# Gate stage woven with a longer row of dense matmuls, and query and key projections in two passes over the tokens, in a two-layer attention and mLSTM encoder

## The chip, the cores and the metric

The kernel runs on one core of one Trainium2 chip. The metric is the device time of one execution in microseconds (us). The core's engines work side by side, each through its own list of instructions in a fixed order: PE (matrix products, with PEld for the loads of its stationary operand), DVE and ACT (elementwise work), POOL, and SP, which here issues DMA transfers. An instruction that waits holds back everything behind it on its engine.

## The reference

Two batches, 256 sample tokens and 512 prompt tokens, pass through two layers with shared weights. Each layer runs differential attention and a bidirectional mLSTM side by side on one input projection, then an output projection, a layer norm, and a gated feed-forward part with a second layer norm. The part that matters here:

```python
aq, ak, av, lq, lk, lv, lo, lg = _split_cols(x @ w_in)
att = _diff_attention(aq, ak, av, lam)                     # 4 heads, 2 score maps each
gates = (lg + gate_bias).reshape(B, S, 4, LSTM_HEADS)
ig_f, lf_f = gates[0], jax.nn.log_sigmoid(gates[1])        # forward; gates 2 and 3 backward
h = _mlstm_direction(q, k, v, ig_f, lf_f) + (same, flipped in time)
mixed = concat([att, sigmoid(lo) * head_rmsnorm(h)]) @ w_out
```

`_mlstm_direction` needs, from the gates, running sums and running maxima along the tokens (a scan), per chunk of 128 tokens.

## The kernel before

All 768 tokens lie in one activation tile, `actA`, the 256 sample tokens first, in six token tiles of 128. Each fp32 product is made of three passes over a high and a low part, so one tile of a dense projection with 1024 input features is 8 x 3 = 24 matmuls.

A layer's first half, the mixer, goes through these stages:

- `lstm_in`: the projections of the mLSTM's queries, keys and gates (`c1a`, `c1b`).
- `gates`: a long chain of small steps, nearly all on DVE and ACT. PE comes in three times: it transposes the gate values (`gT`, L474), spreads 64 values over partitions with a small product (`aB`, L517), and transposes the results back (`colT`, L524, four groups).
- `dense("av")`: the attention's values, six tiles of 24 matmuls of 512 columns. `dense("lv")` and `dense("lo")` are of the same form, for the mLSTM's values and output gates.
- `att_in(h)`: query and key projection of head h. `feat_major` (L347) makes 24 pairs of matmuls, each with one stationary weight block: 256 columns for the sample tokens (into `aqkB`), 512 for the prompt tokens (into `aqkA`). One PSUM tile `pB` holds the sample part of the queries in its first half and of the keys in its second.
- `att(h)`: per block of 128 queries two score products (`s`), a reduction on DVE, two exponentials on ACT, a combination on DVE, transposes (`aT`) and the product with the values (`u`).
- `lstm_states` and `lstm_out`: the mLSTM proper. `lstm_decay` loads the decay tiles `pt` (L570) and `qet` (L577) from DRAM through SP, after the gate stage has written their source there, adds a mask on DVE (L572) and takes exponentials on ACT (L574).

What stands beside what is written by hand. `weave` takes one step (up to the next `yield`) of the generator that is least far along, by the step counts given to it:

```python
weave((gates(), 8), (dense("av", ev_av), 7))
weave((att_in(0), 3))
weave((att(0), 7, PR_A), (dense("lv", ev_lv), 7, PR_LO))
```

The framework's scheduler then makes each engine's final order from this program order and the priorities. Weights come as raw pieces (`raw`, six buffers), and are converted into two parts (`wh` on ACT, L171; `wl` on DVE, L172) in twelve slots. A conversion waits until the last matmul that used its slot is done, and the load of a raw piece waits until the piece that had its buffer is converted.

Of the kernel before, what the change touches and what calls it, by code (L numbers as in the profile page):

```python
# [20 lines left out]
SA, SB = 512, 256  # L21
T = SA + SB
# [24 lines left out]
PR_A = 0  # L47
PR_L = 0
PR_LO = 10
# [156 lines left out]
def trunk(ctx, nc, tc, d, o, depth=DEPTH):  # L206
    V, S, G, PE = nc.vector, nc.scalar, nc.gpsimd, nc.tensor
# [18 lines left out]
    def P(tag, name):  # L226
        return pp.tile([128, 512], F32, tag=tag, name=name, bufs=banks[tag])
# [118 lines left out]

    def feat_major(blocks, psA, psB):  # L347

        n = 0
        for k in range(8):  # L350
            _, h, l = blocks[k // 4]
            for a, b in PASSES:
                w = (h, l)[a][:, (k % 4) * 128:(k % 4 + 1) * 128]
                PE.matmul(psB, w, actA[:, k, b, 0:SB], start=n == 0, stop=n == 23)  # L354
                PE.matmul(psA, w, actA[:, k, b, SB:T], start=n == 0, stop=n == 23)  # L355
                n += 1

    def transposed_split(src, name, tag, hi, lo):

# [8 lines left out]
    for l in range(depth):  # L368
# [28 lines left out]
        def dense(tag, evac):  # L397
            units = [W.take() for _ in range(8)]
            for t in range(NT):
                p = P("d", f"{tag}{t}")  # L400
                tok_major(t, units, p, slice(0, 512))
                evac(t, p)
                yield
            W.done(*units)
# [23 lines left out]
        def gates():  # L428
# [38 lines left out]
            t2 = gp.tile([128, T], F32, name="t2")  # L467
            mpe = gp.tile([64, 2, 6], F32, name="mpe")
            ae = gp.tile([64, 6], F32, name="ae")
            for c0, c1 in ((0, 4), (4, 6)):  # L470
                ps = P(TAG_GT, f"gT{c0}")
                n = (c1 - c0) * 128
                for t in range(c0, c1):
                    PE.transpose(ps[:, (t - c0) * 128:(t - c0 + 1) * 128], gs[:, t].rearrange("p a b c -> p (a b c)"), ident)  # L474
                S.copy(ig[:, c0 * 128:c1 * 128], ps[0:64, :n])
                V.tensor_copy(lf[:, c0 * 128:c1 * 128], ps[64:128, :n])
# [35 lines left out]
            V.tensor_tensor(out=v6(t2[64:128]), in0=v6(t1[0:64]), in1=me.unsqueeze(2).to_broadcast([64, 6, 128]), op=ALU.subtract)  # L512
            V.tensor_tensor(out=ae, in0=mp, in1=me, op=ALU.subtract)
            S.activation(ae, ae, AF.Exp)
            ps = P(TAG_GT, "aB")
            for i in range(4):
                PE.matmul(ps[:, i * 6:(i + 1) * 6], sel[:, i, :], ae, start=True, stop=True)  # L517
# [148 lines left out]
        def att_in(h):  # L666
            qs = 0.125 * 2.0 ** (8.0 * (h + 1) / 4)
            uq, uk = [[W.take(), W.take()] for _ in range(2)]
            pB = P("d", f"aqkB{h}")
            lo_, hi_ = slice(0, 64), slice(64, 128)  # L670
            for ui, uu in ((0, uq), (1, uk)):
                pA = P("d", f"aqkA{h}{ui}")
                pBu = pB[:, ui * 256:(ui + 1) * 256]
                feat_major(uu, pA, pBu)
                W.done(*uu)
                for ps, tk in ((pBu, slice(0, SB)), (pA, slice(SB, T))):
                    if ui == 0:
                        S.activation(sQ[lo_, 0, tk], ps[lo_], AF.Identity, scale=qs)
                        S.activation(sQ[hi_, 1, tk], ps[hi_], AF.Identity, scale=qs)
                        V.scalar_tensor_tensor(out=sQ[hi_, 0, tk], in0=ps[lo_], scalar=qs, in1=sQ[lo_, 0, tk].bitcast(F32), op0=ALU.mult, op1=ALU.subtract)  # L680
                        V.scalar_tensor_tensor(out=sQ[lo_, 1, tk], in0=ps[hi_], scalar=qs, in1=sQ[hi_, 1, tk].bitcast(F32), op0=ALU.mult, op1=ALU.subtract)
                    else:
                        S.copy(sK[lo_, 0, tk], ps[lo_])
                        S.copy(sK[hi_, 1, tk], ps[hi_])
                        S.copy(sK[hi_, 0, tk], ps[lo_])
                        S.copy(sK[lo_, 1, tk], ps[hi_])
                        V.tensor_tensor(out=kL[lo_, 0, tk], in0=ps[lo_], in1=sK[lo_, 0, tk].bitcast(F32), op=ALU.subtract)
                        V.tensor_tensor(out=kL[hi_, 1, tk], in0=ps[hi_], in1=sK[hi_, 1, tk].bitcast(F32), op=ALU.subtract)
                yield
# [49 lines left out]
        def weave(*gens):  # L739

            live = [[0, n, i, g, (*o, 0)[0]] for i, (g, n, *o) in enumerate(gens)]
            while live:
                e = min(live, key=lambda e: ((e[0] + 0.5) / e[1], e[2]))
                e[0] += 1
                with prio(e[4]):
                    done = next(e[3], live) is live
                if done:
                    live.remove(e)

        def chain(*gens):  # L750
            for g in gens:
                yield from g
# [3 lines left out]
            late_constants()  # L756
        G.iota(dneg, [[-1, 896]], base=384, channel_multiplier=1, allow_small_or_imprecise_dtypes=True)
        V.scalar_tensor_tensor(out=dneg, in0=dneg, scalar=-1.0, in1=dneg, op0=ALU.mult, op1=ALU.min)
        weave((gates(), 8), (dense("av", ev_av), 7))
        CPX = ExitStack()  # L760
        lc = CPX.enter_context(tc.tile_pool(name=f"lc{l}", bufs=1, reuse_waits="tile"))
        weave((att_in(0), 3))
        weave((att(0), 7, PR_A), (dense("lv", ev_lv), 7, PR_LO))
        lo = dense("lo", ev_lo)
        weave((chain(att_in(1), att(1)), AT1, PR_A), (chain(lstm_states(lc), *[lstm_out(lc, c) for c in range(OUTS)]), 4 * OUTS + 9, PR_L), *([(islice(lo, L1), L1 + W1)] if L1 else []))
        weave((chain(att_in(2), att(2)), AT2, PR_A), (chain(*[lstm_out(lc, c) for c in range(OUTS, NT)]), 4 * (NT - OUTS) + 1, PR_L), *([(islice(lo, L2), L2 + W2, PR_LO)] if L2 else []))
# [331 lines left out]
```

## Time and profile before

| | |
|---|---|
| three runs | 1855.55, 1855.73 (median), 1857.43 us |
| profiled execution | 1855.45 us, of which 1853.7 us are the span of the trace |
| busy share | PE 97%, PEld 86%, DVE 72%, ACT 41%, POOL 13% |
| granted PE clock over the span | 0.992 |
| chain that ended last, by engine | PE 78%, DVE 13%, ACT 5% |

The profiled execution is one of the same kernel, 0.3 us below the median of the runs. The span runs from the first to the last instruction; the remaining 1.75 us lie around it. A clock of 1.00 is PE's upper level, 2.4 GHz; the lower level, 1.2 GHz, would show as 0.50, and a window's figure is the mean over it.

### The profile page before, as it was taken

How to read it: one execution, taken by the hardware profiler on the slowest of the kernel's cores; microseconds unless marked ns; L12 is line 12 of the kernel's file. 1: busy time of each engine (PE TensorE's matmuls, PEld its weight loads, DVE VectorE, ACT ScalarE, POOL GpSimd, SP SyncE). 2: the span in 40 equal slices, each digit the busy share in tenths (PEclk: the TensorE clock that was granted, in tenths of full speed). 3: DMA queues.
4: the chain of work that ended last, by engine and by line, in shares of the span. 5: the costliest groups of instructions: out<-in, count | busy, mean ns of one | idle time of the engine just before them, and what ended most of it. 6: DMA issues, size and time to landing. Idle time of an engine off the chain costs nothing.

```text
span 1853.7 us, 26256 instructions
## 1 busy us (share of the span) xinstructions
PE 1804.3 (97%) x9692; PEld 1587.1 (86%) x9692; DVE 1340.4 (72%) x2576; ACT 768.9 (41%) x1624; POOL 241.9 (13%) x260
## 2 busy tenths in 40 slices
PE   8899999999999999999998999999999999999998
PEld 8778777789899899899897787777898998998996
DVE  5434787589887786787954457775898877877878
ACT  4344576425343343343332455672353343343340
POOL 2000111041111111110120011011411111111102
PEclk9999999999999999999999999999999999999999
DMA  6232110402322222122322121104022221221211
GB/s 190 67 79 69 35 58 24 159 18 69 92 74 69 64 74 68 64 75 86 101 96 83 42 69 52 46 25 170 2 90 80 80 79 47 80 76 51 80 63 68
DMA packets 83280, 134.95 MB, mean 73 GB/s; under 512 B 7984, under 2 KB 27056, under 8 KB 83152
## 3 DMA queue, kind: packets, MB, share of 16 engines
q1 hardware_dynamic: 82432, 132.90, 22.7%
q8 instruction: 76, 1.25, 0.3%
q14 instruction: 52, 0.43, 0.1%
q10 hardware_dynamic: 720, 0.37, 0.1%
HBM read 126.86 MB, written 6.39 MB: 72 GB/s over the span
## 4 chain that ended last, share of the span: by engine, by line
PE 78%; DVE 13%; ACT 5%; issue 2%; POOL 2%; DMA 1%; SPq 0%; DVEq 0%; ACTq 0%; POOLq 0%
PE p L921 32%; PE dn L981 16%; PE wo L877 5%; PE aqkA L355 3%; PE lv L345 3%; PE lo L345 3%; PE aqkB L354 2%; DVE wl L172 2%; PE c1a L345 2%; PE u L724 2%; PE av L345 2%; PE c1b L345 2%; PE num L618 1%; ACT wh L171 1%; PE num L614 1%
## 5 line engine op out<-in xcount | busy, mean ns | idle before, releaser
L921 PE MATMUL p<-actA,wh 128*128 128x384 f32 x1408 | 363.4, 338 | 3.2 <-DVE g L946 3.2
L171 ACT ACTIVATE wh<-raw 128x512 fp32r<-128x512 f32 (+1 forms) x348 | 215.5, 629 | 303.3 <-PE p L921 110.2
L172 DVE TENSOR_TENSOR wl<-raw,wh 128x512 fp32r<-128x512 f32 (+1 forms) x348 | 243.2, 708 | 96.9 <-ACT wh L171 96.4
L921 PE MATMUL p<-actB,wh 128*128 128x384 f32 x1056 | 270.0, 337 | 0.0
L921 PEld LDWEIGHTS p<-actA,wh 128*128 128x128 f32 x1408 | 254.7, 188 | 5.8 <-DVE g L946 3.8
L921 PE MATMUL p<-actA,wl 128*128 128x384 f32 x704 | 237.3, 337 | 0.0
L149 POOL TENSOR_TENSOR T<-raw,raw 128x512 f32<-128x512 f32 x88 | 120.5, 1371 | 837.0 <-DVE wl L172 525.7
L981 PE MATMUL dn<-wh,actB 128*128 128x512 f32 x576 | 208.8, 396 | 1.1 <-DVE acc L988 1.1
L171 ACT ACTIVATE wh<-T 128x512 fp32r<-128x512 f32 x176 | 108.4, 628 | 221.3 <-DVE acc L988 104.9
L921 PEld LDWEIGHTS p<-actB,wh 128*128 128x128 f32 x1056 | 191.3, 188 | 0.0
L981 PE MATMUL dn<-wh,ring 128*128 128x512 f32 x480 | 179.1, 396 | 1.6 <-DVE acc L988 1.6
L921 PE MATMUL p<-actB,wl 128*128 128x384 f32 x528 | 177.2, 336 | 0.0
L988 DVE TENSOR_TENSOR acc<-acc,dn 128x512 f32<-128x512 f32 x144 | 98.1, 681 | 72.0 <-PE dn L981 71.7
L172 DVE TENSOR_TENSOR wl<-T,wh 128x512 fp32r<-128x512 f32 x176 | 129.6, 748 | 22.0 <-ACT wh L171 21.9
L981 PEld LDWEIGHTS dn<-wh,actB 128*128 128x128 f32 x576 | 108.0, 188 | 29.8 <-DVE acc L988 2.8
L921 PEld LDWEIGHTS p<-actA,wl 128*128 128x128 f32 x704 | 132.2, 188 | 0.1
L877 PE MATMUL wo<-wh,actB 128*128 128x512 f32 x384 | 122.7, 396 | 0.0
L981 PE MATMUL dn<-wl,actB 128*128 128x512 f32 x288 | 113.2, 393 | 0.0
L981 PEld LDWEIGHTS dn<-wh,ring 128*128 128x128 f32 x480 | 90.0, 188 | 24.6 <-DVE acc L988 4.2
L921 PEld LDWEIGHTS p<-actB,wl 128*128 128x128 f32 x528 | 99.1, 188 | 0.0
L355 PE MATMUL aqkA<-actA,wh 128*128 128x512 f32 x256 | 98.8, 408 | 0.0
L981 PE MATMUL dn<-wl,ring 128*128 128x512 f32 x240 | 94.5, 394 | 0.0
(265 smaller groups left out, 3412.5 us busy)
## 6 DMA issues: line engine op xcount, KB each, us to landing
raw<-in_w_g_dram SPq DMA_DIRECT2D x88, 256.0 KB, 2.8
raw<-in_w_u_dram SPq DMA_DIRECT2D x88, 256.0 KB, 2.8
raw<-in_w_down_dram SPq DMA_DIRECT2D x88, 256.0 KB, 2.8
raw<-in_w_out_dram SPq DMA_DIRECT2D x32, 256.0 KB, 2.6
pt<-scr_m SPq DMA_DIRECT2D x12, 512.0 KB, 6.2
raw<-in_w_c_dram SPq DMA_DIRECT2D x16, 264.0 KB, 3.6
raw<-in_w_av_dram SPq DMA_DIRECT2D x16, 256.0 KB, 4.1
raw<-in_w_aq_dram SPq DMA_DIRECT2D x16, 256.0 KB, 3.7
```

Of the source, the lines that this page charges most:

```text
L149: src["engine"].tensor_tensor(out=src["tile"], in0=a, in1=b, op=ALU.subtract)
L171: self.nc.scalar.activation(h, v, AF.Identity)
L172: self.nc.vector.tensor_tensor(out=l, in0=v, in1=h.bitcast(F32), op=ALU.subtract)
L345: PE.matmul(ps, xh(k, t, a), (h, l)[b][:, cols], start=k + i == 0, stop=k == 7 and i == 2)
L354: PE.matmul(psB, w, actA[:, k, b, 0:SB], start=n == 0, stop=n == 23)
L355: PE.matmul(psA, w, actA[:, k, b, SB:T], start=n == 0, stop=n == 23)
L614: PE.matmul(pn[:, di * 256:di * 256 + 129], qet[r, di, hh // 2, :], cst[di, c][r, hh // 2, :], start=di == dirs[0], stop=False, skip_group ...
L724: PE.matmul(pu[:, qt * 128:(qt + 1) * 128], aT[:, st * 128:(st + 1) * 128], av[:, s0 + st, h * 128:(h + 1) * 128], start=st == 0, stop=st ...
L877: PE.matmul(p, actB[:, k, a, t * 128:(t + 1) * 128], units[k][1 + b], start=n + i == 0, stop=n == 7 and i == 2)
L921: PE.matmul(ps, blk[1 + a][:, k * 128:(k + 1) * 128], x[:, k, b, :], start=k + i == 0, stop=k == 3 and i == 2)
L981: PE.matmul(p, x, (wh_, wl_)[b], start=k + i == 0, stop=k == nf - 1 and i == 2)
L988: V.tensor_tensor(out=z, in0=z, in1=p, op=ALU.add)
```

## The change

`feat_major` makes two passes: first the 24 matmuls of the sample tokens, then the 24 of the prompt tokens, with the same stationary blocks in the same order. `gates` gets two more `yield`s, one ahead of the `gT` transposes and one ahead of `aB`. Its partner in the weave is now a chain: all of `av`, then `att_in(0)`, then the first tile of `lv`. The next weave has what is left of `lv`, five tiles. The pool `lc`, in which the decay tiles lie, is still opened after the gate stage's pool is closed, which is now after `att_in(0)` in program order.

```diff
--- before.py
+++ after.py
@@ -346,14 +346,14 @@
 
     def feat_major(blocks, psA, psB):
 
-        n = 0
-        for k in range(8):
-            _, h, l = blocks[k // 4]
-            for a, b in PASSES:
-                w = (h, l)[a][:, (k % 4) * 128:(k % 4 + 1) * 128]
-                PE.matmul(psB, w, actA[:, k, b, 0:SB], start=n == 0, stop=n == 23)
-                PE.matmul(psA, w, actA[:, k, b, SB:T], start=n == 0, stop=n == 23)
-                n += 1
+        for ps, tok in ((psB, slice(0, SB)), (psA, slice(SB, T))):
+            n = 0
+            for k in range(8):
+                _, h, l = blocks[k // 4]
+                for a, b in PASSES:
+                    w = (h, l)[a][:, (k % 4) * 128:(k % 4 + 1) * 128]
+                    PE.matmul(ps, w, actA[:, k, b, tok], start=n == 0, stop=n == 23)
+                    n += 1
 
     def transposed_split(src, name, tag, hi, lo):
 
@@ -467,6 +467,7 @@
             t2 = gp.tile([128, T], F32, name="t2")
             mpe = gp.tile([64, 2, 6], F32, name="mpe")
             ae = gp.tile([64, 6], F32, name="ae")
+            yield
             for c0, c1 in ((0, 4), (4, 6)):
                 ps = P(TAG_GT, f"gT{c0}")
                 n = (c1 - c0) * 128
@@ -512,6 +513,7 @@
             V.tensor_tensor(out=v6(t2[64:128]), in0=v6(t1[0:64]), in1=me.unsqueeze(2).to_broadcast([64, 6, 128]), op=ALU.subtract)
             V.tensor_tensor(out=ae, in0=mp, in1=me, op=ALU.subtract)
             S.activation(ae, ae, AF.Exp)
+            yield
             ps = P(TAG_GT, "aB")
             for i in range(4):
                 PE.matmul(ps[:, i * 6:(i + 1) * 6], sel[:, i, :], ae, start=True, stop=True)
@@ -756,11 +758,11 @@
             late_constants()
         G.iota(dneg, [[-1, 896]], base=384, channel_multiplier=1, allow_small_or_imprecise_dtypes=True)
         V.scalar_tensor_tensor(out=dneg, in0=dneg, scalar=-1.0, in1=dneg, op0=ALU.mult, op1=ALU.min)
-        weave((gates(), 8), (dense("av", ev_av), 7))
+        lv = dense("lv", ev_lv)
+        weave((gates(), 10), (chain(dense("av", ev_av), att_in(0), islice(lv, 1)), 10))
         CPX = ExitStack()
         lc = CPX.enter_context(tc.tile_pool(name=f"lc{l}", bufs=1, reuse_waits="tile"))
-        weave((att_in(0), 3))
-        weave((att(0), 7, PR_A), (dense("lv", ev_lv), 7, PR_LO))
+        weave((att(0), 7, PR_A), (lv, 6, PR_LO))
         lo = dense("lo", ev_lo)
         weave((chain(att_in(1), att(1)), AT1, PR_A), (chain(lstm_states(lc), *[lstm_out(lc, c) for c in range(OUTS)]), 4 * OUTS + 9, PR_L), *([(islice(lo, L1), L1 + W1)] if L1 else []))
         weave((chain(att_in(2), att(2)), AT2, PR_A), (chain(*[lstm_out(lc, c) for c in range(OUTS, NT)]), 4 * (NT - OUTS) + 1, PR_L), *([(islice(lo, L2), L2 + W2, PR_LO)] if L2 else []))
```

No instruction is added or taken away on any engine; the change is one of order, and it reaches from the gate stage to the start of the output projection (`wo`) in each layer. Both layers get the same order, but for a few rows (before, 19 of the 24 matmuls of the first `av` tile stood ahead of `gT` in layer 0, and 22 in layer 1; now all 24 do in both). The places below are those of layer 0.

**First place: PE in the gate stage, at `aB`.** `av2`, `av3`, `av4` are tiles of the value projection. Before:

```order
L345 MATMUL av2_784<-wl25_573,actA_70 128x512
L345 MATMUL av2_784<-wh25_572,actA_70 128x512
L345 MATMUL av2_784<-wh26_578,actA_70 128x512
L517 MATMUL aB_778<-ae_686,sel_636 128x6 x4
L345 MATMUL av2_784<-wl26_579,actA_70 128x512
L345 MATMUL av2_784<-wh26_578,actA_70 128x512
L345 MATMUL av2_784<-wh27_584,actA_70 128x512
```

and after:

```order
L345 MATMUL av3_804<-wh28_590,actA_70 128x512
L345 MATMUL av3_804<-wl28_591,actA_70 128x512
L345 MATMUL av3_804<-wh28_590,actA_70 128x512
L519 MATMUL aB_830<-ae_686,sel_636 128x6 x4
L345 MATMUL av4_836<-wh21_188,actA_70 128x512
L345 MATMUL av4_836<-wl21_189,actA_70 128x512
L345 MATMUL av4_836<-wh21_188,actA_70 128x512
```

Before, `aB` stands inside the third value tile, after 16 of its 24 matmuls; now it stands between the fourth and the fifth, and the `gT` transposes, which were inside the first and second tile, come after the first and inside the second.

**Second place: PE in the projections of head 0.** `aqkA00` and `aqkA01` are the prompt parts of queries and keys, `aqkB0` the tile with both sample parts; the suffixes of wh and wl name weight blocks. Before, at the step from queries to keys:

```order
L354 MATMUL aqkB0_962<-actA_70,wh30_602 128x256
L355 MATMUL aqkA00_963<-actA_70,wh30_602 128x512
L354 MATMUL aqkB0_962<-actA_70,wl30_603 128x256
L355 MATMUL aqkA00_963<-actA_70,wl30_603 128x512
L355 MATMUL aqkA01_1032<-actA_70,wh31_608 128x512 x2
L355 MATMUL aqkA01_1032<-actA_70,wl31_609 128x512
L355 MATMUL aqkA01_1032<-actA_70,wh31_608 128x512 x2
L355 MATMUL aqkA01_1032<-actA_70,wl31_609 128x512
L355 MATMUL aqkA01_1032<-actA_70,wh31_608 128x512
L354 MATMUL aqkB0_962<-actA_70,wh31_608 128x256 x2
```

and after, at the step from the sample pass to the prompt pass of the queries:

```order
L355 MATMUL aqkB0_949<-actA_70,wl30_603 128x256
L355 MATMUL aqkB0_949<-actA_70,wh30_602 128x256 x2
L355 MATMUL aqkB0_949<-actA_70,wl30_603 128x256
L355 MATMUL aqkA00_950<-actA_70,wh29_596 128x512 x2
L355 MATMUL aqkA00_950<-actA_70,wl29_597 128x512
L355 MATMUL aqkA00_950<-actA_70,wh29_596 128x512 x2
```

Before, sample and prompt matmuls alternate and both tiles end together; now the sample tile ends 24 prompt matmuls earlier. The keys' sample pass follows the queries' prompt pass, and the first `lv` tile follows the keys' prompt pass as a whole (before, the first scores stood inside it).

**Third place: ACT and SP around the decay tiles.** ACT before:

```order
L171 ACTIVATE wh41_1012<-raw41_926 128x512
L574 ACTIVATE pt0_1834<-pt0_1834,cols_239 128x128 x5
L678 ACTIVATE sQ_228<-aqkB0_962 64x256
L679 ACTIVATE sQ_228<-aqkB0_962 64x256
L678 ACTIVATE sQ_228<-aqkA00_963 64x512
L679 ACTIVATE sQ_228<-aqkA00_963 64x512
L171 ACTIVATE wh42_1018<-raw42_932 128x512
L574 ACTIVATE pt0_1834<-pt0_1834,cols_239 128x128 x3
L171 ACTIVATE wh43_1081<-raw43_938 128x512
L574 ACTIVATE pt1_1856<-pt1_1856,cols_239 128x128 x8
```

and ACT after, where `tp000` are the exponentials of the first attention block:

```order
L533 ACTIVATE cols_239<-colT41_1096 128x2x8 x2
L576 ACTIVATE pt0_1834<-pt0_1834,cols_239 128x128 x5
L412 COPY vaug_237<-lv0_1101 128x4x128
L576 ACTIVATE pt0_1834<-pt0_1834,cols_239 128x128
L716 ACTIVATE tp000_1135,sm000_1134<-tp000_1135,mn000_1136 128x256
L716 ACTIVATE tp000_1135,cc000_1137<-tp000_1135,mn000_1136 128x256
L576 ACTIVATE pt0_1834<-pt0_1834,cols_239 128x128 x2
L576 ACTIVATE pt1_1856<-pt1_1856,cols_239 128x128 x7
L724 COPY aT000_1154<-aT000_1151 128x256
```

The decay exponentials stood between two key conversions and ahead of the evacuation of the queries (`sQ`); now they stand behind both projections and ahead of the first attention block. DVE's order has moved in the same way: the two mask additions of `pt0` stand directly ahead of the reductions of `tp000`, and the first of `pt1` between these and the combination that `aT000` waits for.

SP's list of DMA transfers, before:

```order
L140 DMA raw45_950<-in_w_aq_dram 128x512
L140 DMA raw46_956<-in_w_aq_dram 128x512
L570 DMA pt0_1834<-scr_m 128x8x128
L577 DMA qet0_1846<-scr_e 64x4x128 x2
L140 DMA raw47_1016<-in_w_ak_dram 128x512
L570 DMA pt1_1856<-scr_m 128x8x128
```

and after:

```order
L140 DMA raw46_947<-in_w_aq_dram 128x512
L140 DMA raw47_1003<-in_w_ak_dram 128x512
L140 DMA raw48_1009<-in_w_ak_dram 128x512
L140 DMA raw49_1076<-in_w_lo_dram 128x512
L572 DMA pt0_1834<-scr_m 128x8x128
L140 DMA raw50_1082<-in_w_lo_dram 128x512
L579 DMA qet0_1846<-scr_e 64x4x128 x2
L572 DMA pt1_1856<-scr_m 128x8x128
```

The load of `pt0` stood behind `raw46` and now stands behind `raw49`, and `pt1` behind `raw50` and both loads of `qet0`.

## Rows read from the trace of the kernel before

**Rows 1.** The page, part 1: busy time of each engine, its share, its instructions.

```profile
PE 1804.3 (97%) x9692; PEld 1587.1 (86%) x9692; DVE 1340.4 (72%) x2576; ACT 768.9 (41%) x1624; POOL 241.9 (13%) x260
```

**Rows 2.** Busy time by window: span, busy (count) per engine, PEclk, DMA, GB/s.

```profile
90.60:114.00 23.40, 19.97 (x100) 17.14 (x98) 8.24 (x14) 10.01 (x29) 0.00 (x0) 0.85 0.63 164
161.40:240.00 78.60, 78.19 (x487) 63.23 (x487) 51.45 (x151) 41.00 (x119) 9.96 (x13) 1.00 0.21 64
240.00:337.00 97.00, 94.27 (x546) 75.17 (x544) 76.10 (x230) 70.25 (x206) 11.52 (x14) 1.00 0.14 44
1012.20:1036.00 23.80, 21.31 (x108) 17.77 (x107) 9.56 (x17) 12.58 (x34) 0.00 (x0) 0.93 0.59 163
```

**Rows 3.** Waits of PE, layer 0, 45 to 340 us: total, times, longest.

```profile
PE aB L517 <- ACT ae L514: 5.3, 1, 5.3
PE aqkB L354 <- DVE sQ L681: 3.4, 1, 3.4
```

**Rows 4.** Waits of PE, layer 1, 966 to 1262 us.

```profile
PE aqkB L354 <- DVE sQ L681: 2.4, 1, 2.4
PE gT L474 <- DVE gs L461: 1.2, 1, 1.2
```

**Rows 5.** Timeline of PE, layer 0: start, length, engine, line, operation, [idle before].

```profile
45.19 0.40 PE L345 MATMUL av<-wh,actA 128*128 128x512 f32 x1
...
50.55 0.63 PE L474 MATMUL gT<-ident,gs 128*128 128x128 f32 x4 [0.80 <-DVE gs L461]
50.94 0.48 PE L345 MATMUL av<-wl,actA 128*128 128x512 f32 x1
...
67.11 1.84 PE L517 MATMUL aB<-ae,sel 64*128 64x6 f32 x8 [5.26 <-ACT ae L514]
...
69.47 1.05 PE L345 MATMUL av<-wh,actA 128*128 128x512 f32 x2
...
113.97 0.39 PE L345 MATMUL lv<-wh,actA 128*128 128x512 f32 x1
```

**Rows 6.** Timeline of PE, layer 1.

```profile
966.81 0.39 PE L345 MATMUL av<-wh,actA 128*128 128x512 f32 x1
...
989.80 1.84 PE L517 MATMUL aB<-ae,sel 64*128 64x6 f32 x8 [5.25 <-ACT ae L514]
...
1033.25 0.40 PE L345 MATMUL lv<-wh,actA 128*128 128x512 f32 x1
```

**Rows 7.** The chain of work that ended last: start, length, step.

```profile
36.64 2.84 PE c1b L345 x24
...
73.28 5.55 PE av L345 x24
...
93.04 7.22 DMA pt<-scr_m
```

**Rows 8.** Timeline of DVE, layer 0.

```profile
51.83 0.69 DVE L476 COPY lf<-gT 64x512 f32<-64x512 f32 x1 [1.43 <-ACT ig L475]
...
100.39 1.29 DVE L572 TENSOR_TENSOR pt<-pt,tri 128x512 f32<-128x512 f32 x2 [4.22 <-DMA pt<-scr_m]
```

**Rows 9.** Timeline of ACT, layer 0.

```profile
66.75 0.21 ACT L514 ACTIVATE ae<-ae 64x6 f32<-64x6 f32 x1
...
101.16 1.57 ACT L574 ACTIVATE pt<-pt,cols 128x128 f32<-128x128 f32 x5 [5.72 <-DVE pt L572]
...
118.27 0.51 ACT L714 ACTIVATE tp<-tp,mn 128x256 f32<-128x256 f32 x1
```

**Rows 10.** The page, parts 5 and 6: weight conversions, loads of the decay tiles.

```profile
L171 ACT ACTIVATE wh<-raw 128x512 fp32r<-128x512 f32 (+1 forms) x348 | 215.5, 629 | 303.3 <-PE p L921 110.2
L172 DVE TENSOR_TENSOR wl<-raw,wh 128x512 fp32r<-128x512 f32 (+1 forms) x348 | 243.2, 708 | 96.9 <-ACT wh L171 96.4
...
pt<-scr_m SPq DMA_DIRECT2D x12, 512.0 KB, 6.2
```

**Rows 11.** Timeline of SP's DMA queue, layer 0.

```profile
93.52 1.73 SPq L577 DMA_DIRECT2D qet<-scr_e  x2
```

## The prediction

> **What bounds the kernel now.** The page comes first: PE is busy for 97% of the span and DVE for 72% [rows 1]. A change of order can only gain where PE stands still or runs at a lower clock, so the next view is the list of PE's waits in each mixer. In layer 0 it has two large entries: 5.3 us at `aB`, behind the exponential on ACT that ends the gate chain, and 3.4 us at the keys' sample matmul, behind DVE's evacuation of the queries [rows 3]. Layer 1 has the same places with 5.25 us [rows 6] and 2.4 us, and 1.2 us at `gT` [rows 4]. The windows show the second cost. The projections of head 0 ran at a mean clock of 0.85 in layer 0 and 0.93 in layer 1 [rows 2], so part of each window, after the wait, was at 1.2 GHz. After the wait at `aB` it is the same: two 512-column matmuls take 1.05 us [rows 5], where an undisturbed tile of 24 takes 5.55 us, 0.231 each [rows 7]. The later mixer is nearly full: PE is busy 78.19 of 78.60 us and 94.27 of 97.00 us [rows 2]. What can be gained lies between the first `av` matmul and the first `lv` matmul.
>
> How much, follows from that stretch as a whole. It lasts 113.97 - 45.19 = 68.8 us in layer 0 [rows 5] and 1033.25 - 966.81 = 66.4 us in layer 1 [rows 6]. Its PE work is the same before and after: six `av` tiles of 5.55 us are 33.3; two projections, each 24 matmuls of 512 columns (5.55) and 24 of 256 columns (2.84, the price of a `c1b` tile), are 16.8 [rows 7]; 18 transposes at 0.39 us for four (50.55 to 50.94) are 1.8; the `aB` matmuls held PE for 67.11 to 68.87 at the lower clock [rows 5], so 0.9 at the upper one. The sum is 52.8 us. So 16.0 us in layer 0 and 13.6 us in layer 1 are waits and half clock.
>
> **The change, part by part.** No instruction is added or removed; every term is a wait that goes, comes or stays.
>
> *The wait at `aB`.* In layer 0 the gate chain runs from 51.83 (the copy `lf`) to 66.96 (the end of `ae`), 15.1 us on DVE and ACT [rows 8, 9]. PE now reaches `aB` after four whole `av` tiles and the `gT` transposes: 45.19 + 4 x 5.55 + 0.6 = 68.0. The chain starts up to 0.6 us later than before, since an `av` evacuation now stands ahead of the gate copies on ACT (bounds: 0 and one 512-column ACT operation, 0.63 [rows 10]; I take 0.4). `ae` then ends at 67.4, 0.6 us ahead of PE. In layer 1 the chain and the tiles are the same, and both start from the same late `gT`, so the margin is alike. The wait goes, and the half clock after it. What covers the chain are 32 matmuls of `av` that stood behind `aB`; if the margin fails, the price is the shortfall alone, under 1 us.
>
> *The wait at `gT`.* It goes in layer 0, where five `av` matmuls now run ahead of the transposes; about 0.3 us may be left ahead of the second group. In layer 1 only two more `av` matmuls run ahead of it than before (22 of 24 did already), which cover 0.5 us; 0.7 of the 1.2 us stay [rows 4].
>
> *The wait at the keys' sample matmul.* It came from two things: both tiles of the queries ended together, and the queries' evacuation stood on ACT behind the decay exponentials, which waited for their load (ACT stood still 5.72 us ahead of `pt` at 101.16 [rows 9]). Now the sample tile ends 5.55 us before the prompt tile, its evacuation is four half-width operations of under 0.7 us each, and no decay work stands ahead of it. The wait goes, with its half clock, in both layers.
>
> *Sum of these.* 16.0 - 0.3 = 15.7 us in layer 0 and 13.6 - 0.7 = 12.9 in layer 1: 28.6 us.
>
> *A new wait, at the first attention block.* The decay work has not gone; it moved with the queues. Call X the end of PE's projections, when `lv0` begins. SP has `pt0` behind `raw49`, whose buffer comes free with the conversion that waits for the first half of the keys' prompt pass. That is X - 2.8; two conversions of 0.63 and 0.71 [rows 10] and a DMA issue later, `pt0` is issued at X - 0.8. It lands after 6.2 (the median [rows 10]) to 7.2 us (the one on the chain [rows 7]), at X + 5.4 to 6.4. On DVE its two mask additions (1.29 together [rows 8]) stand ahead of the reductions of the first block, and on ACT five decay exponentials (1.57 [rows 9]), the evacuation of `lv0` (0.6) and one more (0.3) stand ahead of its two exponentials (0.51 each [rows 9]). That chain gives about X + 9.8 to 10.8 for the exponentials. `pt1` is issued behind `raw50` (waiting for the last keys matmul, X + 2) and two `qet0` loads (1.73 together [rows 11]) at X + 3.7; it lands at X + 9.9 to 10.9, and its first mask addition stands on DVE ahead of the combination. With both mask additions and the combination (some 2.2 us) the transposes `aT000` can start at X + 12.1 to 13.1. PE meanwhile has `lv0` (5.55), four score matmuls (0.5) and 16 matmuls of `lv1` (3.7): it is there at X + 9.8. So it stands still for 2.3 to 3.3 us, nearly the size of the two waits that went (2.4 and 3.4). Their half clock cost (1 - 0.85) x 23.4 = 3.5 us and (1 - 0.93) x 23.8 = 1.7 us [rows 2]. Together 4.0 to 6.8 us a layer. I take 5.2, so 10.4 us are given back. Lower bound: 0, if the loads land some 3 us earlier than I work out.
>
> *The rest of the mixer.* One `lv` tile less lies beside the attention of head 0; its last block is covered by the queries' sample pass of head 1 instead, and later blocks stand 1 to 2 us earlier in PE's work than before. PE's total is unchanged and its stages had only 0.4 and 2.7 us idle [rows 2], so I take 0; the upper bound is the price of one more wait like that at the keys, 3.4 + 3.5 = 6.9 us a layer.
>
> Sum against the profiled execution: 1855.45 - 28.6 + 10.4 = 1837.3 us. The median of the runs shown lies 0.3 us above that execution, so **1838 us** (rounded up), about 1.0% faster.
>
> One point speaks against the two passes. Each weight block serves two neighbouring matmuls before and matmuls 24 apart after, so if one load served both, the change would add 24 loads in each of 16 projections, 384. The page's row excludes that: PEld has 9692 loads for 9692 matmuls [rows 1], so each matmul already loads its own, and a run of 256-column matmuls goes at 2.84 us for 24 [rows 7] with those loads beside it. Were the loads shared and exposed, 384 x 1587.1/9692 = 0.164 us would be 63 us. The Trainium skill (TensorE: Matmul & The Clock Gate, Step-by-step: what each phase is for) says that weights typically stay put across many matmuls, so that one load serves several; with its estimate of columns / 1.2 ns for a load (LDWEIGHTS section) the sum would be 41 us slower, but this trace does not have the shared loads.
>
> **The rivals.**
>
> *Nothing is given back.* The decay loads land early enough, or `lv1` covers them. For it: the loads of `pt` now start without a wait for the gate chain, and 2 to 3 us is a small margin of a 13 us chain. Against it: in both layers this load held up ACT and DVE before. Time: 1855.7 - 28.6 = 1827 us.
>
> *More waits later.* The attention of heads 1 to 3 loses the slack that `lv0` gave. For it: the window with the least slack has DVE at 76.10 and ACT at 70.25 of 97.00 us [rows 2]. Against it: the same work stands there and PE was short of work only 2.7 us. Time: 1838 plus up to 13.8, 1845 to 1852 us.
>
> *Slower.* The decay loads become the bound. DVE and ACT hold the whole attention of head 0 behind `pt0` and `pt1`, so each microsecond by which `pt1` lands later is one of PE's. To end 0.2% slower the give-back must be 28.6 + 3.7 = 32.3 us, 16 a layer, which is reached when `pt1` lands some 10 us later than worked out, 16 us after issue where 6.2 to 7.2 were seen. Time: 1860 us and more.
>
> *The change does not do what it says.* `ae` comes later than PE in its new place as well, or the projections lose what they share. Time: 1850 to 1857 us in the first case.
>
> **How the numbers follow.** The forecast, 1833 to 1844 us, has 0.56; nothing given back 0.17; more waits later 0.18; the change without effect 0.05; slower 0.03, shared loads 0.01. A range from 1827 to 1849 leaves out slower, no effect, and the outer parts of the two neighbours, about 0.18. What a measurement of this kernel can tell from no change is 0.2%, 3.7 us. Faster by more than that is 0.56 + 0.17 + 0.15 = 0.88, within it 0.07, slower 0.05.
>
> **What would show it.** The list of PE's waits in the profile after should have no entry at `aB` and none at the keys' sample matmul. The stretch from the first `av` matmul to the first `lv` matmul should be near 53 us in both layers, at a clock of 1.00. A wait of 2 to 3 us should stand at the first `aT`, with DVE or ACT as its releaser and the load of `pt` behind that, and after it matmuls at half pace. I am wrong if that wait is missing (then about 1827 us), if it is above 6 us, or if the windows of heads 1 to 3 show PE idle for more than 5 us a layer where they had 3.

## The result and the profile after

The changed kernel takes 1832.3 us (median of four runs, 1831.4 to 1834.1) where the kernel before took 1856.6 beside it (1855.6 to 1857.6): a ratio of 0.987, 95% interval 0.9853 to 0.9887, so 1.3% faster. The span of the trace fell from 1853.7 to 1830.8 us. In the changed kernel the lines behind the edits stand one or two higher: `gT` is L475, `aB` L519, the decay's load L572 and mask L574, `aT` L722, `aoT` L738, and both projections L355.

The page, part 1, answers to [rows 1]. PE's busy time fell by 9 us with the same number of instructions: the work is the same, and less of it ran at half clock.

```profile
PE 1795.5 (98%) x9692; PEld 1579.8 (86%) x9692; DVE 1343.3 (73%) x2576; ACT 768.4 (42%) x1624; POOL 241.7 (13%) x260
```

The mixer is cut at the same three matmuls in both traces: the first `av`, the first `lv`, the first of the output projection (`wo`). First the kernel before, the two stretches of layer 0 and the two of layer 1; the columns are those of [rows 2].

```profile
45.19:113.97 68.78, 59.29 (x268) 48.69 (x267) 30.55 (x54) 25.00 (x57) 1.19 (x2) 0.90 0.34 97
113.97:334.46 220.49, 217.51 (x1251) 173.56 (x1250) 148.78 (x439) 130.86 (x377) 21.26 (x27) 1.00 0.14 44
966.81:1033.25 66.44, 57.66 (x269) 47.34 (x267) 31.04 (x55) 26.27 (x60) 1.19 (x2) 0.92 0.34 100
1033.25:1253.64 220.39, 217.46 (x1251) 173.50 (x1250) 148.79 (x439) 130.87 (x377) 21.24 (x27) 1.00 0.14 44
```

And the changed kernel:

```profile
45.65:98.85 53.20, 53.20 (x268) 44.12 (x267) 29.32 (x52) 21.41 (x43) 1.63 (x2) 1.00 0.28 92
98.85:321.30 222.45, 218.08 (x1253) 173.62 (x1252) 151.73 (x441) 134.47 (x392) 21.07 (x27) 1.00 0.17 51
953.67:1007.84 54.17, 53.48 (x268) 44.09 (x267) 29.71 (x53) 22.86 (x46) 1.64 (x2) 1.00 0.28 90
1007.84:1231.36 223.52, 218.13 (x1253) 173.56 (x1252) 151.80 (x441) 134.59 (x392) 20.87 (x27) 1.00 0.17 50
```

Read the first figure behind each window. The gate stretch is shorter by 15.6 us in layer 0 and 12.3 in layer 1, together 27.9. Its clock is 1.00, and PE is busy in all of it but 0.7 us at `gT` in layer 1. The stretch behind it is longer by 2.0 and 3.1 us, together 5.1. The rest of the program moves by less than 1 us, and the span falls by 22.9.

Where the 5.1 us are, the waits of PE say. Layer 0 of the changed kernel, from `lv` to `wo`:

```profile
PE aoT L738 <- DVE ao L734: 1.0, 1, 1.0
PE aT L722 <- DVE tp L719: 0.8, 1, 0.8
```

Layer 1, with the gate stage:

```profile
PE aoT L738 <- DVE ao L734: 1.2, 2, 1.0
PE aT L722 <- DVE tp L719: 1.1, 1, 1.1
PE num L616 <- DVE pt L602: 1.0, 1, 1.0
PE aoT L738 <- DVE cc L717: 0.8, 1, 0.8
PE gT L475 <- DVE gs L461: 0.7, 1, 0.7
```

The entries of [rows 3] and [rows 4] at `aB` and `aqkB` are gone, and `gT` in layer 1 fell from 1.2 to 0.7. New are `aT` (0.8 and 1.1; layer 0 had 0.2 there before), the last `aoT` of head 0 (1.0 and 1.2) and, in layer 1, `num` (1.0): 5.1 us in all. That this is just what the two stretches lost is in part chance: the entry at `cc` grew from 0.6 to 0.8 in both layers, one at the scores fell from 0.9 to 0.6, and PE's busy time in the two windows rose by 0.6 and 0.7 us.

PE's timeline of layer 0 answers to [rows 5]:

```profile
45.65 0.40 PE L345 MATMUL av<-wh,actA 128*128 128x512 f32 x1
...
68.66 1.05 PE L519 MATMUL aB<-ae,sel 64*128 64x6 f32 x8
69.64 0.50 PE L345 MATMUL av<-wh,actA 128*128 128x512 f32 x1
...
90.24 0.48 PE L355 MATMUL aqkB<-actA,wh 128*128 128x256 f32 x2
...
98.85 0.48 PE L345 MATMUL lv<-wh,actA 128*128 128x512 f32 x1
...
109.64 0.44 PE L722 MATMUL aT<-ident,tp 128*128 128x128 f32 x2 [0.81 <-DVE tp L719]
109.83 0.48 PE L345 MATMUL lv<-wl,actA 128*128 128x512 f32 x1
```

`aB` has no idle time before it and takes 1.05 us where it took 1.84. `ae` on ACT began at 67.42 and took 0.21 us, 1.0 us ahead of PE:

```profile
67.42 0.21 ACT L515 ACTIVATE ae<-ae 64x6 f32<-64x6 f32 x1
```

The keys' first sample matmul, at 90.24, has no idle time before it either. The first `aT` waits 0.81 us, and the matmul behind it is at full pace.

Behind that wait stand the decay's loads. SP's queue and then DVE, layer 0:

```profile
97.71 0.43 SPq L572 DMA_DIRECT2D pt<-scr_m  x1
...
101.88 0.60 SPq L572 DMA_DIRECT2D pt<-scr_m  x1
```

```profile
103.20 1.29 DVE L574 TENSOR_TENSOR pt<-pt,tri 128x512 f32<-128x512 f32 x2
...
107.58 0.69 DVE L574 TENSOR_TENSOR pt<-pt,tri 128x512 f32<-128x512 f32 x1 [1.87 <-DMA pt<-scr_m]
108.18 0.16 DVE L717 RECIPROCAL cc<-cc 128x1 f32<-128x1 f32 x1
108.26 0.67 DVE L574 TENSOR_TENSOR pt<-pt,tri 128x512 f32<-128x512 f32 x1
108.85 0.21 DVE L718 SCALAR_TENSOR_TENSOR cc<-sm,nlam,cc 128x1 f32<-128x1 f32 x1
109.09 0.49 DVE L719 SCALAR_TENSOR_TENSOR tp<-tp,cc 128x256 f32<-128x256 f32 x1
```

The first load was there within 5.5 us of its issue (97.71 to 103.20; the mask had no wait for it), the second after 5.7 (101.88 to 107.58). DVE waited 1.87 us for the second, with the attention's combination (L719) queued behind it. That is the place and the mechanism that were forecast, at a third of the size.

### The profile page after: what moved, and what is told of

It reads as the page before. It is cut to its first block, busy times and chain, and to the rows that moved or that the text cites. A ratio compares the mean times of both kernels' runs of the same rounds, so it can differ in the third digit from the quotient of the medians.

```text
span 1830.8 us, 26258 instructions
## 1 busy us (share of the span) xinstructions
PE 1795.5 (98%) x9692; PEld 1579.8 (86%) x9692; DVE 1343.3 (73%) x2576; ACT 768.4 (42%) x1624; POOL 241.7 (13%) x260
## 4 chain that ended last, share of the span: by engine, by line
PE 80%; DVE 12%; ACT 2%; POOL 2%; issue 2%; DMA 1%; SPq 0%; DVEq 0%; POOLq 0%; ACTq 0%
PE p L923 32%; PE dn L983 16%; PE wo L879 5%; PE aqkA L355 4%; PE av L345 3%; PE lo L345 2%; PE lv L345 2%; PE aqkB L355 2%; DVE wl L172 2%; PE u L726 2%; PE c1a L345 2%; PE c1b L345 2%; PE num L620 1%; PE num L616 1%; PE s L710 1%
## 5 line engine op out<-in xcount | busy, mean ns | idle before, releaser
L879 PEld LDWEIGHTS wo<-wh,actB 128*128 128x128 f32 x384 | 71.8, 188 | 16.2
```

The lines of the kernel that those rows point to most:

```text
L879: PE.matmul(p, actB[:, k, a, t * 128:(t + 1) * 128], units[k][1 + b], start=n + i == 0, stop=n == 7 and i == 2)
```

## The experiments

My theory after the result: the row (the dense work that is woven with the gate stage) gains by covering the gate chain, which needs both its length and the two stops (the added `yield`s), and by moving the decay behind the projections; the 5 us given back are small waits at both ends of head 0's attention. The rivals: the two parts of the change each carry their own share; or the row's `lv` tile is what matters.

**The projections' order alone.**

The kernel before (e1) with this alone:

```diff
-                PE.matmul(psB, w, actA[:, k, b, 0:SB], ...)
-                PE.matmul(psA, w, actA[:, k, b, SB:T], ...)
+        for ps, tok in ((psB, slice(0, SB)), (psA, slice(SB, T))):
...
+                    PE.matmul(ps, w, actA[:, k, b, tok], ...)
```

> The kernel before with only the projections' new order (sample tokens first, then prompt tokens); the gate stage stays woven with the short row. My sum's theory, in which the two parts of the change are worth what their own waits cost: the keys' sample matmul no longer waits for the queries' evacuation behind the decay's exponentials (3.4 us in the first layer, 2.4 in the second) nor runs on at half clock after it, the wait at aB (5.3 us a layer) stays: about 11 us faster than before, 1843 to 1848 us. Rival A, the wait only moves on, to the first scores, which need the keys' differences that VectorE makes behind the decay's masks: within 4 us of before, 1852 to 1857 us. Rival B, the longer row carries all of the gain and this order nothing: 1855 to 1857 us.

Measured: 1850.9 us (1848.3 to 1852.9) beside 1857.4 of before, ratio 0.9966 (0.9953 to 0.9978), a gain of 6.5 us. It is neither figure: less than the two waits with their half clock, more than nothing. The waits of layer 0 show why:

```profile
PE aB L517 <- ACT ae L514: 5.3, 1, 5.3
PE aT L720 <- DVE tp L717: 2.2, 1, 2.2
```

The wait at `aqkB` is gone in both layers, and 2.2 and 2.1 us now stand at the first `aT` instead. The 11 us of the first theory less these 4.3 are 6.7, close to the 6.5 measured. So rival A was right that part of it moves on, and wrong about the place. The new wait is not one for the decay's loads. DVE had finished their masks at 107.5, and the combination (L717) stands behind the differences of the keys' prompt part (`kL`), which wait for ACT's evacuations:

```profile
106.78 0.69 DVE L572 TENSOR_TENSOR pt<-pt,tri 128x512 f32<-128x512 f32 x1
...
113.79 0.68 DVE L687 TENSOR_TENSOR kL<-aqkA,sK 64x512 fp32r<-64x512 f32 x1 [1.39 <-ACT sK L686]
114.48 0.69 DVE L688 TENSOR_TENSOR kL<-aqkA,sK 64x512 fp32r<-64x512 f32 x1
...
115.66 0.48 DVE L717 SCALAR_TENSOR_TENSOR tp<-tp,cc 128x256 f32<-128x256 f32 x1
```

**The row and the stops without the projections' order.**

This is the changed kernel (e2) with the edit of e1 taken back:

```diff
-        for ps, tok in ((psB, slice(0, SB)), (psA, slice(SB, T))):
...
-                    PE.matmul(ps, w, actA[:, k, b, tok], ...)
+                PE.matmul(psB, w, actA[:, k, b, 0:SB], ...)
+                PE.matmul(psA, w, actA[:, k, b, SB:T], ...)
```

> The changed kernel with only the projections' old order put back (the matmuls of sample and prompt tokens alternate); row and gate steps as changed. In the changed kernel's trace the decay's first mask and exponentials stand behind all evacuations of the projections, so theory one: the wait at the keys' sample matmul was an effect of the decay standing ahead, and with the longer row it is gone whatever the projections' order: 1832 to 1836 us, with no wait above 1 us there. Theory two, in which the new order itself carries the share of that wait (some 11 us in two layers): 1841 to 1845 us, with waits of 2 to 3 us at the keys' first sample matmul.

Measured: 1832.8 us (1832.4 to 1833.6), ratio 0.9871 (0.9858 to 0.9885). Theory one. The only entry at the keys' sample matmul is 0.4 us in layer 1. With the longer row the projections' order is worth nothing that can be measured; without it, it was worth 6.5 us.

**The row without the stops, and the stops without the row.**

The first (e3) is an edit of the changed kernel, the second (e4) of the kernel before.

```diff
-            yield
...
-            yield
...
-        weave((gates(), 10), (chain(dense("av", ev_av), att_in(0), islice(lv, 1)), 10))
+        weave((gates(), 8), (chain(dense("av", ev_av), att_in(0), islice(lv, 1)), 10))
```

> The changed kernel without the two added stops in the gate stage, woven 8 to 10 rather than 10 to 10; aB then stands behind 72 dense matmuls rather than 96. Theory one, the wait at aB goes because aB stands behind more work: PE comes there 24 matmuls (5.5 us) earlier than in the changed kernel, at about 63.1 us in the first layer, while its operand is ready at about 67.5: a wait of 3.5 to 4.5 us in each layer and half clock behind it, 1842 to 1847 us. Rival, the longer row alone does it, since it moves the operand's chain too: 1832 to 1834 us.

```diff
+            yield
...
+            yield
...
-        weave((gates(), 8), (dense("av", ev_av), 7))
+        weave((gates(), 10), (dense("av", ev_av), 7))
```

> The kernel before with only the two added stops in the gate stage (10 to 7, the row without the projections), the projections in the old order. aB stands behind 72 dense matmuls rather than 64. Theory one: its wait shrinks by those 8 matmuls, 1.8 us a layer, and the gT wait goes (0.3 and 0.7 us), but what is gained there PE waits longer at the keys' sample matmul, since the decay that it waits for is not moved: 1852 to 1856 us. Rival, the stops by themselves are worth a large part of the change: under 1847 us.

Measured: without the stops 1847.8 us (ratio 0.9951, 0.9938 to 0.9965), with the stops alone 1852.4 (0.9976, 0.9966 to 0.9987). Without the stops, PE's timeline of layer 0 shows:

```profile
67.79 1.84 PE L517 MATMUL aB<-ae,sel 64*128 64x6 f32 x8 [4.59 <-ACT ae L514]
69.55 0.80 PE L345 MATMUL av<-wh,actA 128*128 128x512 f32 x1
70.15 0.63 PE L345 MATMUL av<-wl,actA 128*128 128x512 f32 x1
```

The wait is back with half pace behind it, and `av` to `lv` takes 60.93 and 62.31 us where the changed kernel takes 53.20 and 54.17: 15.9 us, where the times differ by 15.6. Of these 9.1 are the two waits (4.6 and 4.5) and 6.7 the half clock, of which I had allowed less; so theory one holds and its range was 1 us short.

With the stops alone `aB` still waits 4.6 and 4.5 us, 0.7 less than before and not 1.8 as theory one had it, and the keys' sample matmul 2.9 and 3.1 us (3.4 and 2.4 before). The median lies in theory one's range, but no execution is near it: of ten, five took 1849.8 to 1850.5 us at a mean clock of 0.995 to 0.996, and five 1854.4 to 1857.0 us at 0.991 to 0.992. The trace is of the first five and has no half clock behind the keys' waits (the last section has the rows); of the others there is none. So the stops alone gain some 7 us or some 2, 5.0 by the median, the row without stops (with the new projections) 9.5, both 24.5. They do not add up, because `aB` waits until both have put 96 matmuls ahead of it; either alone puts 72.

**No decay loads, and the loads earlier.**

Both (e5, then e9) are edits of the changed kernel, in `lstm_decay`; the arguments of the load are left out.

```diff
-            nc.sync.dma_start(pt, ...)
+            if c < 2:
+                G.memset(pt, 0.0)
+            else:
+                nc.sync.dma_start(pt, ...)
```

> The changed kernel with the first two decay tiles of each layer set to zero by GpSimd instead of loaded from DRAM (two 512 KB loads a layer are left out, so the decay of the first two token tiles is not the reference's). Theory one, the wait at the first attention transpose (0.8 and 1.1 us) is behind these loads, above all the second, for which VectorE waited 1.9 us ahead of the combination: that wait is below 0.4 us in both layers and the time 1829.5 to 1831.8 us. Rival, the wait is the attention's own chain of exponentials and combination: it stays at 0.8 to 1.1 us, 1832 to 1833 us.

```diff
-            nc.sync.dma_start(pt, ...)
+            with prio(600 if c < 2 else 0):
+                nc.sync.dma_start(pt, ...)
```

> The changed kernel with the second decay load issued right behind the first on SP's queue, ahead of a weight load and the two small loads (about 3.5 us earlier, at 98.2 us rather than 101.9 us in the first layer). Theory one, the second load is late and holds VectorE ahead of the combination: VectorE's wait for it (1.9 us) goes, the wait at the first attention transpose falls below 0.5 us, 1830 to 1832 us. Rival, the two 512 KB loads share the DMA engines, so the first lands later by as much, or the masks now stand ahead of the scores' minima: the wait at the transpose stays or grows, 1832 to 1835 us.

Measured: 1831.0 us (1830.7 to 1831.2) without the loads, 1831.5 (1830.2 to 1832.7) with both first. Without them, the first `aT` waits 0.3 us in both layers, and that behind 11 matmuls of the second `lv` tile rather than 16, since the scheduler put it earlier; theory one. With the loads first, the mask of the second ran directly behind that of the first:

```profile
102.54 2.50 DVE L575 TENSOR_TENSOR pt<-pt,tri 128x512 f32<-128x512 f32 x4
```

Both 512 KB loads, issued from 97.06 us on, were thus in place within some 6 us, as they are one by one (5.5 and 5.7), and `aT` waits 0.5 us in both layers. The time of e9 can't be told from the changed kernel's. Here the first `aT` stands behind 13 matmuls of the second `lv` tile. The 5 and 3 matmuls by which it stands earlier in the two runs, at 0.23 us each, are more than the wait that is left, so behind 16 it would not have waited: in the changed kernel the loads are behind all of the `aT` wait, and that is 1 to 2 us of 1832.

None of the runs so far, nor the next two, had the changed kernel beside it. The kernel before took 1857.4 and 1857.6 us beside them, 0.8 and 1.0 more than beside the changed kernel, so a difference of 1 us from 1832.3 says little.

**The row's length.**

One `lv` tile less than the changed kernel has in the row (e8), and one more (e10):

```diff
-        weave((gates(), 10), (chain(dense("av", ev_av), att_in(0), islice(lv, 1)), 10))
+        weave((gates(), 10), (chain(dense("av", ev_av), att_in(0)), 9))
...
-        weave((att(0), 7, PR_A), (lv, 6, PR_LO))
+        weave((att(0), 7, PR_A), (lv, 7, PR_LO))
```

> The changed kernel with the row one tile shorter: the first lv tile is not done in the gate stage's row but stays beside head 0's attention, which then has 6 of them; woven 10 to 9. Theory one, the tile in the row only moves cover from one end of the attention to the other: the wait of about 1.0 us a layer at the last aoT of head 0, where the changed kernel has no lv matmuls left, goes; the first attention transpose, with the same matmuls ahead of the combination's exponentials but no finished lv tile, waits 1 to 2.5 us a layer: 1831 to 1835 us. Rival, the lv tile in the row is what covers the decay's loads, and without it the first transposes wait 4 us or more a layer, with half clock behind: 1840 us or more.

```diff
-        weave((gates(), 10), (chain(dense("av", ev_av), att_in(0), islice(lv, 1)), 10))
+        weave((gates(), 10), (chain(dense("av", ev_av), att_in(0), islice(lv, 2)), 10))
...
-        weave((att(0), 7, PR_A), (lv, 6, PR_LO))
+        weave((att(0), 7, PR_A), (lv, 5, PR_LO))
```

> The changed kernel with two lv tiles rather than one in the gate stage's row, 4 left beside head 0's attention. Theory one, more finished lv work lies ahead of the first attention transpose, so that its wait (0.8 and 1.1 us) goes, and what is taken from the end of head 0's attention is missing there: the waits at aoT and beside head 0's last tiles grow by 2 to 6 us a layer, 1834 to 1842 us. Rival, the work taken from the end costs nothing more than the 1.0 us that is waited at the last aoT already: 1830 to 1832 us.

Measured: 1829.9 us for either (1829.3 to 1831.1 and 1828.9 to 1830.6), ratios 0.9853 (0.9839 to 0.9868) and 0.9852 (0.9837 to 0.9867). Both lie below theory one's range. Without the `lv` tile the first `aT` waits 0.6 us in both layers, in layer 1 a further one 0.8 (I expected 1 to 2.5 a layer), and `aoT` 0.3: the tile in the row is not what covers the decay's loads. With two tiles the waits of layer 0 are these, and `aT` is not among them:

```profile
PE aoT L738 <- DVE ao L734: 1.3, 2, 1.0
PE aoT L738 <- DVE cc L717: 0.8, 1, 0.8
```

The missing tile at the end costs nothing beyond the 1.0 us that stood there already; my price of 2 to 6 us a layer was wrong, the rival right.

**The last `lv` tile later.** The changed kernel ran here again, with no edit, beside two variants: e11 is e10 with a slower weave, e12 the changed kernel with one.

> The changed kernel itself once more, beside the two variants of it that run here: 1831 to 1834 us, as it was measured; no theory differs.

```diff
-        weave((att(0), 7, PR_A), (lv, 5, PR_LO))
+        weave((att(0), 7, PR_A), (lv, 4, PR_LO))
```

> Two lv tiles in the row, as in the run with two of them, and the four that are left woven into head 0's attention at a slower rate (7 to 4), so that the last one is done at the attention's end. Theory one, the changed kernel's two give-backs are separate, the first transpose's wait (0.8 and 1.1 us) for want of finished work ahead of it, the last aoT's wait (1.0 us a layer) for want of work beside it, and either is worth its own wait: both gone, 1827.0 to 1829.0 us, 0.2% under the changed kernel. Rival, the earlier blocks of head 0 that now share three lv tiles wait in place of the last one: 1830 us or more.

```diff
-        weave((att(0), 7, PR_A), (lv, 6, PR_LO))
+        weave((att(0), 7, PR_A), (lv, 5, PR_LO))
```

> The changed kernel with only the weave of head 0's attention and the five left lv tiles at a slower rate (7 to 5 rather than 7 to 6). Theory one: the wait at the last aoT (1.0 us a layer) goes and the first transpose's stays, 1830.0 to 1831.5 us. Rival, what leaves the early blocks makes them wait: 1832 us or more.

Measured: the changed kernel 1832.3 us (1831.7 to 1832.8), e11 1829.0 (1828.6 to 1830.4), e12 1829.2 (1828.8 to 1829.6). The runs of either variant and of the changed kernel do not overlap; they are 0.18% and 0.17% faster, less than the 0.2% that one comparison can tell. Waits of e12, layer 0:

```profile
PE aT L722 <- DVE tp L719: 1.0, 1, 1.0
...
PE aoT L738 <- DVE ao L734: 0.3, 1, 0.3
```

So the wait at the last `aoT` (1.0 us before) goes when an `lv` tile is kept for it, and the one at `aT` stays: the mechanism of theory one. The block's `aoT` now stands at 149.12 us, inside head 1's sample pass, where it stood at 154.89, inside the prompt pass. The time is 0.8 us under theory one's range, and the gain of 3.1 us is over 1 us more than the `aoT` entries account for. In e11 the time came out as theory one had it and the mechanism, by the trace of its slowest execution (1830.4), did not: `aT` has no wait, but `aoT` waits 1.9 us in layer 0 and 1.8 in layer 1, an earlier block (0.57) now among them. What else e11 gained stays open.

The changed kernel's second profile is worth a look as well. There `aT` waits 1.5 us in layer 0 and not at all in layer 1, where the first had 0.8 and 1.1, and `num` in layer 1 does not wait. DVE's first mask of the second load (`pt1`) shows why `aT` differs. These are layer 1 of the first profile, then layers 0 and 1 of the second:

```profile
1016.87 0.69 DVE L574 TENSOR_TENSOR pt<-pt,tri 128x512 f32<-128x512 f32 x1 [2.14 <-DMA pt<-scr_m]
```

```profile
107.90 0.69 DVE L574 TENSOR_TENSOR pt<-pt,tri 128x512 f32<-128x512 f32 x1 [2.56 <-DMA pt<-scr_m]
...
1016.12 0.69 DVE L574 TENSOR_TENSOR pt<-pt,tri 128x512 f32<-128x512 f32 x1 [0.87 <-DMA pt<-scr_m]
```

With layer 0 of the first profile ahead of them, `pt1` was issued at 101.88, 1010.77, 101.50 and 1011.28, so it was in place 5.7, 6.1, 6.4 and 4.8 us after issue, and `aT` waited 0.8, 1.1, 1.5 and 0 us. The four layers of e3 and e12 fall in line (5.5 to 6.5 us, waits of 0.5 to 1.4). In this order up to some 4.9 us of the load are covered, and each microsecond above that is one of PE's. The same load thus varies by over 1 us from one execution to the next, and the wait with it.

## Why the prediction was right, and where it was off

- *Wait at `aB`, wait at `gT`, wait at the keys, with their half clock: 28.6 us.* Measured 27.9 (15.6 of 15.7, 12.3 of 12.9). `ae` was 1.0 us ahead of PE where I had 0.6. That the stretch as a whole was priced, by its length less PE's work, made this term good: single waits would have missed the half clock. The run without the stops (e3) shows the part that hangs on `aB`, 15.9 us.
- *The keys' wait goes for two reasons.* I named the projections' order and the decay that no longer stands ahead. The run with the old projections (e2) shows that the second is enough; the first does nothing in the changed kernel.
- *A new wait at the first attention block: 10.4 us.* Mechanism and place right, size wrong. With X = 98.85, `pt0` was issued at X - 1.1 (I had X - 0.8) and was in place by X + 4.4 (X + 5.4 to 6.4); `pt1` was issued at X + 3.0 (X + 3.7) and in place at X + 8.7 (X + 9.9 to 10.9); the transposes began at X + 10.8 (X + 12.1 to 13.1), PE stood ready at X + 10.0 (X + 9.8). So the wait was 0.8 us (1.1 in layer 1), not 2.3 to 3.3. The step that failed is the arrival of `pt1`: its issue came 0.7 us earlier than worked out, and the load took 5.7 us, 4.8 to 6.4 in the four cases above, where I took 6.2 to 7.2. The 6.2 had little behind it: of the page's twelve loads the trace shows the landing of one (issued at 1014.60), and the 4.2 on the changed kernel's page is likewise one load, `pt0` of layer 0.
- *Half clock behind that wait, 1.7 to 3.5 us.* There was none, and in e1 none behind a longer wait (below). This part of the term was 0. The price itself was 0.4 us high for layer 0: PE worked at a clock of 0.50 from 104.34 to 110.47, 6.13 us, which costs 3.1; the rest of the 3.5 fell into the wait.
- *The rest of the mixer: 0.* Measured 3.2 us, the 5.1 less the 1.9 at `aT`: mainly `aoT` 1.0 and 1.2, and `num` 1.0. I had counted on the queries' sample pass to cover head 0's last block. It did not: that pass was over at 147.6, ahead of the block's transposes at 148.88. An `lv` tile that is left for it does, as e12 shows. Why `num` waited in one profile and not in the other stays open.

The errors had opposite signs, so it is in part luck that the time is no further off: 8.5 us too much given back at the first block (10.4 against 1.9), 3.2 too little behind it, and 0.7 too much gained ahead of it. The time, 5.7 us under the forecast, lies inside the range (1827 to 1849), just under the forecast's own (1833 to 1844) and above the rival in which nothing is given back (1827). Of the signs that were named, the missing entries and the stretch near 53 us came true (54.2 in layer 1, with the 0.7 left at `gT`); the wait at the first `aT` stood in its place, but not in its size and without half pace behind it. The slower rival was far off, since each load landed earlier and not 10 us later, and shared weight loads showed nowhere: with 9692 loads as before, the stretch in layer 0 is 53.20 us where the sum of the work gave 52.8.

## What to carry to other kernels

Price a stretch that has waits and half clock by its length less the work in it, and then look for what the same transfers will hold up next, since part of a wait can come back behind it: 4.3 of 5.8 us in e1, 1.9 in the changed kernel. When a change has two parts that aim at waits, measure each alone: here one part was worth 6.5 us without the other and nothing with it, and two others 5.0 (2 or 7) and 9.5 us apart but 24.5 together. A load's time on a page can rest on a single transfer; for a wait of a microsecond compare several. Where dense work covers a chain, a tile that is spent early is missing at the other end of the chain that it covered before, so look at the last block as well as at the first.

## What was unexpected of the hardware

The length of a wait does not say whether half clock follows. In the kernel before, layer 1, PE slowed down behind 2.37 us, one matmul pair later (256 columns in 0.21 us each, not 0.12):

```profile
1024.81 0.51 PE L354 MATMUL aqkB<-actA,wh 128*128 128x256 f32 x2 [2.37 <-DVE sQ L681]
1025.15 0.34 PE L354 MATMUL aqkB<-actA,wl 128*128 128x256 f32 x1
1025.29 0.63 PE L354 MATMUL aqkB<-actA,wh 128*128 128x256 f32 x2
```

With the stops alone (e4) the same place in layer 0 waits longer, 2.92 us, and stays at the upper level:

```profile
102.28 0.50 PE L354 MATMUL aqkB<-actA,wh 128*128 128x256 f32 x2 [2.92 <-DVE sQ L683]
102.62 0.28 PE L354 MATMUL aqkB<-actA,wl 128*128 128x256 f32 x1
```

And in e1, behind 2.2 us at `aT`, the granted clock of the next stretch is 1.00:

```profile
109.50:135.00 25.50, 23.31 (x115) 18.27 (x115) 11.17 (x33) 11.78 (x33) 0.72 (x1) 1.00 0.07 22
```

Half clock followed the waits of 3.4 to 5.3 us at `aqkB` and `aB`, and of the five between 2.1 and 3.1 us (one here before, two in e1, two in e4) it followed one. It need not even be the same in two executions of one kernel. The ten of e4 lie in two groups with medians of 1850.2 and 1855.3 us, 5.1 apart, at two mean clocks. In the kernel before, the half clock behind the keys' waits cost 4.8 us (3.1 in layer 0 and, by 3.4 us of work at 0.51, 1.7 in layer 1), so half clock behind these waits in one group and not in the other would account for the gap. That is an estimate from the times, since no trace of the slower group is kept.

What decides between these stays open. The Trainium skill (TensorE: Matmul & The Clock Gate, What's actually happening) says that the chip watches how busy PE has been in a window of time that runs freely and is not reset when a kernel starts, so that the point at which the clock changes shifts; that would fit, but no run here shows it. For a forecast it means that a wait between 2 and 3 us may cost its length alone or nearly twice that.
